# Expert weights split whole or in halves, none multiplied in float32, in a two-layer hybrid decoder trunk

## The chip, the cores and the metric

The kernel runs on one core of one Trainium2 chip. The metric is the device time of one execution in microseconds. The time before is 1491.45 us, the median of 3 runs (1490.14 to 1492.38). All runs are fp32 in and out.

## What is computed

Two layers, each a mixer (differential attention and a gated delta rule side by side), a normalisation, a channel mixer and a normalisation. The first layer's channel mixer is a dense SwiGLU, the second's is the part this document is about: 256 tokens, each sent to 2 of 8 experts.

```python
D_MODEL, SEQ, N_EXPERTS, TOP_K, D_FF_EXPERT = 1024, 256, 8, 2, 3584

def swiglu(x, w_gate, w_up, w_down):
    return (jax.nn.silu(x @ w_gate) * (x @ w_up)) @ w_down

def moe_ffn(x, router_w, w_gate, w_up, w_down):
    logits = jnp.einsum('td,de->te', xf, router_w)
    top_val, top_idx = lax.top_k(logits, TOP_K)
    gates = jax.nn.softmax(top_val, axis=-1)
    ...
    y = swiglu(xb, w_gate[e_b], w_up[e_b], w_down[e_b])
    ...
```

Here `xb` holds the tokens sorted by expert, in blocks that belong to one expert each, and a token's output is the sum of `gate * y` over its two experts.

## The kernel before

**Precision by two parts.** Weights and activations are fp32, and TensorE works on them as pairs of float32r numbers: a high part, which ScalarE (ACT) makes by a copy, and a low part, which VectorE (DVE) makes as the difference. `halves` (L162) does this to a loaded piece of weights: for each half of the piece an ACT copy `wh<-raw` (L177) and a DVE subtraction `wl<-raw,wh` (L180). A product is then x_high·w_high + x_low·w_high + x_high·w_low.

**The expert loop** (`experts`, L980). Each expert's 3584 hidden columns are taken in two chunks of 1792 (`CHUNK`). A chunk needs 8 gate pieces and 8 up pieces of 128 x 1792 (896 KB each) and 7 down pieces of 128 x 2048 (1 MB each). For each chunk the loop multiplies the 8 gate pieces (`in_pieces`, `products`), a few down pieces of the chunk before (`down`, through `more`), applies SiLU to the gate banks (ACT `hh<-ps`, L1194), multiplies the 8 up pieces, again a few down pieces of the chunk before, then DVE multiplies the up banks into `hh` (L1217), and the rest of the down pieces of the chunk before follow. So the down products of a chunk always run inside the chunk that comes after it. TensorE (PE) then transposes `hh` into `hT` (`to_features`, L1125), with one ACT copy and one DVE subtraction for each group of columns.

**Wide and narrow experts.** The experts run in an order by token count: a wide one (up to 128 rows), then narrow and wide in turn for three narrow ones (up to 64 rows, `NARROW = 3`, `TURN`), then two more wide ones. A wide expert multiplies a weight's high part by x_high and x_low and its low part by x_high. A narrow one puts x_high and x_low side by side as 64 + 64 rows, so a piece costs one pass for each part of the weight. The low rows' result then stands in the upper half of the PSUM banks. `leads` (L1114) copies these upper halves on ACT (`room<-ps`), and PE adds them to the lower halves by a product with `shift` (the "moves").

**The last gate and the last up piece of a narrow chunk are not split.** `load(..., whole=True)` puts them in a slot of their own (`ring2`), `as_one` (L1027) has made x in one part, and `products` multiplies them in float32 on the lower 64 rows alone. Since these four products don't touch the upper halves, the `room` copies stand ahead of them:

```python
if narrow and sub[0] == KD - 1:
    subs = next(downs, None)
    moves = leads(banks)
products(banks, xg, narrow, *sub, x32)
```

**Buffers.** Weights land in 7 raw slots (`RING`). The split parts have 4 half-piece buffers in `wpool` and 4 more in `wpool2`, taken in turn, so four pieces can be split ahead.

**What sets the order.** The instructions of each engine run in order. A list scheduler sets it ahead of time, from the order of the program, where nothing is pinned. `side` is a list of small steps, of which one is placed behind each piece: the transposes into `hT`, `combine` (L1088: the copy of an expert's result from PSUM into `ys`, its product with the transposed dispatch matrix `DT`, and the addition into `x_tok`), `transposed` (which makes `DT` from `D`) and `dispatch` (L1003: it gathers the rows of the next one or two experts into `xg`, eight parts, each with PE products into a bank `ps_a` and ACT copies `xg<-ps_a`). The tag `a` has two banks. `ys` and `D` share one buffer.

## Time and profile before

| | |
|---|---|
| median of 3 runs | 1491.45 us (1490.14 to 1492.38) |
| profiled execution | 1492.99 us |
| its span, first to last instruction | 1490.9 us |
| TensorE clock granted, mean | 0.988 |
| PE / PE weight loads / DVE / ACT busy | 1448.6 / 1233.1 / 1218.3 / 1036.6 us |
| HBM read | 431.17 MB, 290 GB/s over the span |

The profile shows one execution. Busy time counts the engine's instructions from start to end with overlaps taken once. Matmuls are pipelined, so PE's busy time overstates the work; the distance from one matmul's start to the next one's says what it costs. The expert loop runs from about 520 us to the end; what comes before it isn't touched by the change.

### The profile page before, as it was taken

The page shows a single profiled execution, that of the slowest core. Times are in us where ns is not written, and L with a number is a line of the kernel's source. Part 1 is how long each engine was busy: PE and PEld are TensorE (multiplying, and loading weights), DVE is VectorE, ACT ScalarE, POOL GpSimd, SP SyncE. Part 2 cuts the span into 40 slices and gives each one's busy share as a digit, 9 for nine tenths or more (in the row PEclk, how much of TensorE's full clock was granted, in tenths as well). Part 3 has the DMA queues.
Part 4 walks back from the last instruction along what each step waited for, and adds up shares of the span by engine and source line. Part 5 has one row for each costly group of instructions (what it writes and reads, how often), then busy time and mean ns, then how long its engine had stood idle before and what let it go on. Part 6 is the DMA issues. An engine that isn't in the chain of part 4 may idle for free.

```text
span 1490.9 us, 24038 instructions
## 1 busy us (share of the span) xinstructions
PE 1448.6 (97%) x8873; PEld 1233.1 (83%) x8873; DVE 1218.3 (82%) x1609; ACT 1036.6 (70%) x1553; POOL 23.7 (2%) x37
## 2 busy tenths in 40 slices
PE   8999999999999999999999999999999999999995
PEld 8978899998987889886698877588877589888884
DVE  6877655556796798989899989899989899989886
ACT  5748544456666587787797887886887877778763
POOL 1100000000000000000000000000000000000000
PEclk9999999999999999999999999999999999999998
DMA  9633455535533179999999999999999899999891
GB/s 322 219 106 118 153 195 195 193 121 196 193 113 100 54 298 363 386 371 374 380 394 384 375 390 394 356 393 408 352 379 417 335 395 413 338 357 395 292 394 34
DMA packets 89124, 433.93 MB, mean 291 GB/s; under 512 B 7816, under 2 KB 9992, under 8 KB 74912
## 3 DMA queue, kind: packets, MB, share of 16 engines
q1 hardware_dynamic: 87808, 428.54, 76.1%
q0 software_dynamic: 1184, 3.71, 0.9%
q8 instruction: 73, 1.20, 0.3%
q14 instruction: 59, 0.48, 0.1%
HBM read 431.17 MB, written 1.05 MB: 290 GB/s over the span
## 4 chain that ended last, share of the span: by engine, by line
PE 87%; DVE 7%; issue 2%; ACT 2%; DMA 0%; DVEq 0%; SPq 0%; ACTq 0%
PE ps_b L99 26%; PE ps_mm L99 25%; PE ps_gd L99 24%; PE ps_a L99 9%; DVE wl L180 4%; PE ps_a L1137 2%; ACT wh L177 1%; DVE x_in L1099 1%; PE ps_mm L566 0%; ACT junk L415 0%; DVE hT L1140 0%; ACT xT L240 0%; PE ps_gd L408 0%; PE ps_mm L670 0%; DVE D L999 0%
## 5 line engine op out<-in xcount | busy, mean ns | idle before, releaser
L180 DVE TENSOR_TENSOR wl<-raw,wh 128x896 fp32r<-128x896 f32 (+2 forms) x851 | 925.7, 1144 | 145.8 <-ACT wh L177 139.4
L177 ACT ACTIVATE wh<-raw 128x896 fp32r<-128x896 f32 (+2 forms) x851 | 792.4, 995 | 153.4 <-PE ps_gd L99 68.4
L99 PE MATMUL ps_b<-wh,hT 128*128 128x512 f32 x816 | 232.6, 396 | 0.7 <-ACT hT L1139 0.7
L99 PE MATMUL ps_gd<-wh,xg 128*128 128x448 f32 x808 | 218.8, 368 | 0.0
L99 PE MATMUL ps_mm<-wh,xg 128*128 128x448 f32 x808 | 212.5, 372 | 0.3
L99 PEld LDWEIGHTS ps_b<-wh,hT 128*128 128x128 f32 x816 | 152.0, 188 | 39.2 <-issue 6.4
L99 PEld LDWEIGHTS ps_gd<-wh,xg 128*128 128x128 f32 x808 | 151.9, 189 | 12.7
L99 PE MATMUL ps_b<-wl,hT 128*128 128x512 f32 x492 | 159.0, 400 | 2.2 <-DVE wl L180 2.2
L99 PEld LDWEIGHTS ps_mm<-wh,xg 128*128 128x128 f32 x808 | 147.6, 189 | 16.4 <-ACT wh L177 2.0
L99 PE MATMUL ps_gd<-wl,xg 128*128 128x448 f32 x488 | 142.9, 374 | 8.9 <-DVE wl L180 7.2
L99 PE MATMUL ps_mm<-wl,xg 128*128 128x448 f32 x488 | 140.7, 369 | 0.1
L99 PEld LDWEIGHTS ps_b<-wl,hT 128*128 128x128 f32 x492 | 90.9, 188 | 31.9 <-DVE wl L180 6.7
L99 PEld LDWEIGHTS ps_gd<-wl,xg 128*128 128x128 f32 x488 | 88.8, 188 | 27.7 <-DVE wl L180 20.2
L99 PEld LDWEIGHTS ps_mm<-wl,xg 128*128 128x128 f32 x488 | 90.9, 188 | 11.7 <-DVE wl L180 4.3
L1139 ACT ACTIVATE hT<-ps_a 128x512 fp32r<-128x512 f32 (+2 forms) x52 | 27.4, 544 | 64.8 <-PE ps_a L1137 37.7
L99 PE MATMUL ps_mm<-xT,wh 128*128 128x256 f32 x448 | 70.9, 280 | 0.0
L99 PEld LDWEIGHTS ps_mm<-xT,wh 128*128 128x128 f32 x448 | 60.8, 189 | 0.4
L1140 DVE TENSOR_TENSOR hT<-ps_a,hT 128x512 fp32r<-128x512 f32 (+2 forms) x52 | 31.8, 621 | 26.5 <-ACT hT L1139 26.5
L99 PE MATMUL ps_gd<-xT,wh 128*128 128x256 f32 x320 | 50.5, 280 | 0.0
L1092 ACT ACTIVATE ys<-ps_b 128x512 fp32r<-128x512 f32 x14 | 8.4, 599 | 53.2 <-PE ps_b L99 39.0
L99 PE MATMUL ps_mm<-xT,wl 128*128 128x256 f32 x224 | 44.6, 280 | 0.0
L99 PEld LDWEIGHTS ps_gd<-xT,wh 128*128 128x128 f32 x320 | 43.1, 189 | 0.0
(407 smaller groups left out, 1660.2 us busy)
## 6 DMA issues: line engine op xcount, KB each, us to landing
raw<-in_moe_w_gate_dram SPq DMA_DIRECT2D x128, 896.0 KB, 8.2
raw<-in_moe_w_up_dram SPq DMA_DIRECT2D x128, 896.0 KB, 6.6
raw<-in_moe_w_down_dram SPq DMA_DIRECT2D x110, 1024.0 KB, 8.1
raw<-in_w_in_dram SPq DMA_DIRECT2D x24, 1024.0 KB, 6.6
raw<-in_ffn_w_gate_dram SPq DMA_DIRECT2D x11, 1024.0 KB, 5.1
raw<-in_ffn_w_up_dram SPq DMA_DIRECT2D x11, 1024.0 KB, 5.1
raw<-in_ffn_w_down_dram SPq DMA_DIRECT2D x11, 1024.0 KB, 4.9
raw<-in_w_out_dram SPq DMA_DIRECT2D x8, 1024.0 KB, 4.9
```

What stands on the lines that cost most here:

```text
L99: return PE.matmul(o, lhsT, rhs, start=start, stop=stop, skip_group_check=True)
L177: high = S.activation(wh[:, c:c + n], w, AF.Copy)
L180: low = V.tensor_tensor(wl[:, c:c + n], w, wh[:, c:c + n].bitcast(F32), op=ALU.subtract)
L1092: S.activation(yh, py[i], AF.Copy)
L1099: V.scalar_tensor_tensor(o, pt, jobs[n][2][:, b], o, op0=ALU.mult, op1=ALU.add)
L1137: PE.transpose(pt[:, f * w:(f + 1) * w], hv[:, f0 + f], ident[rows, rows])
L1139: S.activation(hT[:, f0:f0 + n_, 0], pv, AF.Copy)
L1140: V.tensor_tensor(hT[:, f0:f0 + n_, 1], pv, hT[:, f0:f0 + n_, 0].bitcast(F32), op=ALU.subtract)
```

## The change

- No piece is multiplied in float32: `as_one` and the argument `whole` are gone, and a narrow chunk splits all 16 of its gate and up pieces.
- Every second piece of the expert loop is split in one go: one ACT copy and one DVE subtraction of 1792 or 2048 elements in place of two of half the size (`Whole`). `wpool2` now holds two buffers of 2048 in place of four of 1024. `products` and `down` treat a whole piece with all its high parts first, then its low parts.
- The extra raw slot takes every eighth load or the next gate or up piece after it, in wide and narrow chunks.
- `leads` now stands behind the last piece and behind the split of one down piece, since the last piece now writes the upper rows too.
- `combine` is cut in two: its copies stay behind the gate pieces, and its additions, `transposed` and the next `dispatch` stand behind the up pieces (`carry`). `ys` and `D` get two buffers.

```diff
-    def load(src, nk, cols, parts=1, cut=1, whole=False):
-        pool, size = (extra[0], CHUNK) if whole and extra else (ring, WC)
+    def load(src, nk, cols, parts=1, cut=1):
+        loads[0] += 1
+        pool, size = ring, WC
+        if extra and cols == CHUNK and loads[0] >= 8:
+            pool, size = extra[0], CHUNK
+            loads[0] = 0
...
+    def halves(ld, cut=1, count=2, parts=1):
+        raw, nk, cols = ld
+        if extra and cut == 1 and parts == 1:
+            turn[0] += 1
+            if turn[0] % 2 == 0:
+                n = nk * cols
+                wh = extra[1].tile([P, WC], F32R, tag="wh", name=nm("wh"))
+                wl = extra[1].tile([P, WC], F32R, tag="wl", name=nm("wl"))
+                high = S.activation(wh[:, :n], raw[:, :n], AF.Copy)
+                low = V.tensor_tensor(wl[:, :n], raw[:, :n], wh[:, :n].bitcast(F32), op=ALU.subtract)
+                return Whole((k, wh[:, k * cols:(k + 1) * cols], wl[:, k * cols:(k + 1) * cols]) for k in range(nk))
+        return split(ld, cut, count)
...
-        def products(outs, xg, narrow, k, parts, x32=None):
-            if narrow and k == KD - 1:
-                for i, o in enumerate(outs):
-                    mm(o[0:64], x32, parts[:, i * BANK:(i + 1) * BANK], False, False)
-                return
+        def products(outs, xg, narrow, k, parts):
             for i, (_, wh, wl) in enumerate(parts):
-                o = outs[2 * i:2 * i + 2]
+                m = 4 if isinstance(parts, Whole) else 2
+                o = outs[m * i:m * i + m]
...
-            return [lambda i=i: part(i) for i in range(2)]
+            return [lambda i=i: copy(i) for i in range(2)], [lambda i=i: add(i) for i in range(2)]
...
-                for sub in in_pieces(wg, c, len(first or ()), narrow):
-                    if narrow and sub[0] == KD - 1:
-                        subs = next(downs, None)
-                        moves = leads(banks)
-                    products(banks, xg, narrow, *sub, x32)
+                for sub in in_pieces(wg, c, len(first or ())):
+                    products(banks, xg, narrow, *sub)
...
+                subs = next(downs, None)
+                moves = leads(banks) if narrow else ()
                 more(subs)
...
+                side, carry = carry, []
                 if c == NC - 1 and groups and n + 1 not in xgs:
-                    group = groups.pop(0)
-                    tiles, side = dispatch([jobs[g] for g in group])
-                    xgs.update(zip(group, tiles))
+                    def gather(group=groups.pop(0), side=side):
+                        tiles, steps = dispatch([jobs[g] for g in group])
+                        xgs.update(zip(group, tiles))
+                        side.extend(steps)
+
+                    side.append(gather)
...
                 if pend and pend[1] == NC - 1:
-                    side += combine(pend[0], pend[3], DT)
+                    copies, carry = combine(pend[0], pend[3], DT)
+                    side += copies
                 if c == 0:
-                    side.append(lambda n=n, later=later: later.append(transposed(n)))
+                    carry.append(lambda n=n, later=later: later.append(transposed(n)))
```

The change also moves instructions, since the scheduler orders anew. In all the following places `wh` is a high part of weights. The first is ACT at the end of the gate pieces of the first chunk of the second narrow expert, before:

```order
L177 ACTIVATE wh_9075<-raw_9065 128x896
L177 ACTIVATE wh_9087<-raw_9085 128x1024
L177 ACTIVATE wh_9091<-raw_9085 128x1024
L1121 ACTIVATE room_9095<-ps_mm_8927 64x448
L1121 ACTIVATE room_9095<-ps_gd_8929 64x448
...
L177 ACTIVATE wh_9123<-raw_9121 128x1024
L177 ACTIVATE wh_9127<-raw_9121 128x1024
L177 ACTIVATE wh_9149<-raw_9147 128x1024
L177 ACTIVATE wh_9153<-raw_9147 128x1024
L1194 ACTIVATE hh_9104<-ps_mm_8927 64x448
L1194 ACTIVATE hh_9104<-ps_gd_8929 64x448
```

and after the change:

```order
L198 ACTIVATE wh_8865<-raw_8855 128x896
L180 ACTIVATE wh_8876<-raw_8874 128x2048
L1138 ACTIVATE room_8880<-ps_mm_8715 64x448
L1138 ACTIVATE room_8880<-ps_gd_8717 64x448
...
L198 ACTIVATE wh_8903<-raw_8901 128x1024
L198 ACTIVATE wh_8907<-raw_8901 128x1024
L1209 ACTIVATE hh_8873<-ps_mm_8715 64x448
L1209 ACTIVATE hh_8873<-ps_gd_8717 64x448
...
L180 ACTIVATE wh_8929<-raw_8927 128x2048
```

Between the four `room` copies and the four SiLUs one down piece is split now, where two were before, and the next one stands behind the SiLUs.

The second place is ACT at the start of the gate pieces of that expert's second chunk, before:

```order
L177 ACTIVATE wh_9439<-raw_9429 128x896
L1092 ACTIVATE ys_9503<-ps_b_8509 128x512
L177 ACTIVATE wh_9460<-raw_9458 128x896
L177 ACTIVATE wh_9468<-raw_9458 128x896
L177 ACTIVATE wh_9487<-raw_9485 128x896
L1139 ACTIVATE hT_9406<-ps_a_9447 128x8x64
L177 ACTIVATE wh_9495<-raw_9485 128x896
L1139 ACTIVATE hT_9406<-ps_a_9476 128x6x64
L177 ACTIVATE wh_9516<-raw_9514 128x896
L177 ACTIVATE wh_9524<-raw_9514 128x896
L1092 ACTIVATE ys_9532<-ps_b_8510 128x512
```

and after the change:

```order
L180 ACTIVATE wh_9195<-raw_9193 128x1792
L1156 ACTIVATE hT_9170<-ps_a_9207 128x8x64
L1156 ACTIVATE hT_9170<-ps_a_9236 128x6x64
L1106 ACTIVATE ys_9259<-ps_b_8304 128x512
L198 ACTIVATE wh_9220<-raw_9218 128x896
L198 ACTIVATE wh_9228<-raw_9218 128x896
L1106 ACTIVATE ys_9280<-ps_b_8305 128x512
L180 ACTIVATE wh_9247<-raw_9245 128x1792
```

Both `hT` copies stand ahead of the third gate piece, and on PE their transposes stand among the last down pieces of the chunk before, where they were behind the second and third gate pieces.

The third place is ACT at the end of a wide expert's second chunk, where `dispatch` gathers for the next two experts. Before, the eight parts stand behind the eight up pieces, one each; the last three are:

```order
L177 ACTIVATE wh_8824<-raw_8822 128x1024
L177 ACTIVATE wh_8828<-raw_8822 128x1024
L1023 ACTIVATE xg_8588<-ps_a_8757 128x128
L1023 ACTIVATE xg_8589<-ps_a_8757 128x256
L177 ACTIVATE wh_8846<-raw_8844 128x1024
L177 ACTIVATE wh_8850<-raw_8844 128x1024
L1023 ACTIVATE xg_8588<-ps_a_8786 128x128
L1023 ACTIVATE xg_8589<-ps_a_8786 128x256
L177 ACTIVATE wh_8872<-raw_8870 128x1024
L177 ACTIVATE wh_8876<-raw_8870 128x1024
L1023 ACTIVATE xg_8588<-ps_a_8815 128x128
L1023 ACTIVATE xg_8589<-ps_a_8815 128x256
```

After the change the fourth to the eighth part stand on PE behind the last up piece, the eighth behind one further matmul, and on ACT so:

```order
L1044 ACTIVATE xg_8482<-ps_a_8585 128x128
L1044 ACTIVATE xg_8482<-ps_a_8592 128x128
...
L180 ACTIVATE wh_8666<-raw_8664 128x2048
L1044 ACTIVATE xg_8482<-ps_a_8599 128x128
L1044 ACTIVATE xg_8482<-ps_a_8606 128x128
...
L198 ACTIVATE wh_8684<-raw_8682 128x1024
L198 ACTIVATE wh_8688<-raw_8682 128x1024
L1044 ACTIVATE xg_8482<-ps_a_8613 128x128
```

The eighth part (8613) takes the bank of the sixth (8599), whose copy now stands behind a whole down piece.

## Rows read from the trace of the kernel before

**Rows 1.** Busy time by engine, the whole span (busy us, share, count).

```profile
PE 1448.6 (97%) x8873; PEld 1233.1 (83%) x8873; DVE 1218.3 (82%) x1609; ACT 1036.6 (70%) x1553; POOL 23.7 (2%) x37
```

**Rows 2.** Four chunks in turn, from one multiplication into `hh` to the next.

```profile
core 0: us, PE busy (x) PEld busy (x) DVE busy (x) ACT busy (x) POOL busy (x), PEclk, DMA share, GB/s
849.28:906.91 57.63, 57.37 (x257) 44.63 (x255) 51.16 (x53) 48.76 (x64) 0.00 (x0) 1.00 1.00 395
906.91:965.14 58.23, 55.33 (x227) 38.46 (x227) 51.41 (x57) 44.30 (x59) 0.00 (x0) 1.00 0.93 363
965.14:1018.38 53.24, 53.24 (x256) 46.64 (x255) 50.47 (x51) 43.07 (x52) 0.00 (x0) 1.00 1.00 400
1018.38:1080.39 62.01, 61.46 (x309) 54.45 (x308) 57.99 (x65) 46.70 (x69) 0.00 (x0) 1.00 0.97 373
```

**Rows 3.** Chain that ended last, 849 to 966 us (start us, us, what).

```profile
900.68 1.65 PE ps_mm L99 x4
902.33 1.50 PE ps_gd L99 x4
...
915.57 0.81 PE ps_mm L99 x4
916.38 0.81 PE ps_gd L99 x4
```

**Rows 4.** Timeline of DVE, 849 to 966 us (start, us, instructions, idle before).

```profile
856.26 8.11 DVE L180 TENSOR_TENSOR wl<-raw,wh 128x896 fp32r<-128x896 f32 x8
866.55 0.69 DVE L1140 TENSOR_TENSOR hT<-ps_a,hT 128x512 fp32r<-128x512 f32 x1 [2.19 <-ACT hT L1139]
...
884.95 16.39 DVE L180 TENSOR_TENSOR wl<-raw,wh 128x896 fp32r<-128x896 f32 x16 [2.27 <-ACT wh L177]
902.36 4.63 DVE L180 TENSOR_TENSOR wl<-raw,wh 128x1024 fp32r<-128x1024 f32 x4 [1.02 <-ACT wh L177]
...
916.01 0.69 DVE L1093 TENSOR_TENSOR ys<-ps_b,ys 128x512 fp32r<-128x512 f32 x1 [0.62 <-ACT ys L1092]
...
920.55 0.69 DVE L1140 TENSOR_TENSOR hT<-ps_a,hT 128x512 fp32r<-128x512 f32 x1 [0.60 <-ACT hT L1139]
...
923.10 0.56 DVE L1140 TENSOR_TENSOR hT<-ps_a,hT 128x384 fp32r<-128x384 f32 x1 [0.62 <-ACT hT L1139]
923.93 1.09 DVE L180 TENSOR_TENSOR wl<-raw,wh 128x896 fp32r<-128x896 f32 x1 [0.28 <-ACT wh L177]
...
943.31 17.52 DVE L180 TENSOR_TENSOR wl<-raw,wh 128x1024 fp32r<-128x1024 f32 x17 [3.22 <-ACT wh L177]
```

**Rows 5.** Groups of DVE instructions by shape, 849.28 to 965.14 us (busy, mean | idle).

```profile
L180 DVE TENSOR_TENSOR wl<-raw,wh 128x896 fp32r<-128x896 f32 x56 | 57.5, 1086 | 3.0 <-ACT wh L177 2.6
L180 DVE TENSOR_TENSOR wl<-raw,wh 128x1024 fp32r<-128x1024 f32 x29 | 33.9, 1220 | 5.8 <-ACT wh L177 5.8
```

**Rows 6.** Groups of ACT splits by shape, 560 to 1470 us.

```profile
L177 ACT ACTIVATE wh<-raw 128x896 fp32r<-128x896 f32 x456 | 399.0, 951 | 14.6 <-PE ps_b L99 6.6 <-PE ps_gd L99 3.3 <-PE ps_mm L99 2.9
L177 ACT ACTIVATE wh<-raw 128x1024 fp32r<-128x1024 f32 x223 | 222.1, 1055 | 10.4 <-DMA raw<-in_moe_w_down_dram 4.5 <-PE ps_mm L99 3.0 <-PE ps_gd L99 1.6
```

**Rows 7.** Timeline of ACT, 849 to 966 us.

```profile
865.92 0.60 ACT L1139 ACTIVATE hT<-ps_a 128x512 fp32r<-128x512 f32 x1 [3.20 <-PE ps_a L1137]
...
933.16 0.97 ACT L1121 ACTIVATE room<-ps_mm 64x448 fp32r<-64x448 f32 x2 [2.00 <-PE ps_mm L99]
```

**Rows 8.** Waits of PE and its weight loads in a wide pair, 965.14 to 1080.39 us (total, times, longest).

```profile
PEld ps_b L99 <- DVE wl L180: 1.0, 2, 0.8
...
PE ps_b L99 <- DVE wl L180: 0.5, 1, 0.5
```

**Rows 9.** Timeline of ACT, 1018 to 1081 us.

```profile
1061.95 0.55 ACT L1023 ACTIVATE xg<-ps_a 128x128 fp32r<-128x128 f32 x2 [4.27 <-PE ps_a L99]
```

**Rows 10.** Chain that ended last, by a wide expert's last up pieces and at the tail.

```profile
847.79 0.43 PE ps_a L99 x4
...
1448.76 0.61 ACT hT L1139
```

More of the change, by code (lines that the diff above doesn't have):

```diff
@@ L160, in load, with split @@
         return raw, nk, cols
-    def halves(ld, cut=1, count=2):
+    class Whole(list):
+        pass
+    def halves(ld, cut=1, count=2, parts=1):
+        raw, nk, cols = ld
+        m = nk * cols // count
+        if extra and cut == 1 and parts == 1:
[5 more added lines that the diff above has]
+                high = S.activation(wh[:, :n], raw[:, :n], AF.Copy)
+                if fence_high[0] is not None:
+                    order(high, fence_high[0])
+                low = V.tensor_tensor(wl[:, :n], raw[:, :n], wh[:, :n].bitcast(F32), op=ALU.subtract)
+                if fence[0] is not None:
+                    order(low, fence[0])
+                return Whole((k, wh[:, k * cols:(k + 1) * cols], wl[:, k * cols:(k + 1) * cols]) for k in range(nk))
+        return split(ld, cut, count)
+    def split(ld, cut, count):
         raw, nk, cols = ld
@@ L185, in piece @@
     def piece(src, nk, cols, parts=1, cut=1):
-        return halves(load(src, nk, cols, parts, cut), cut)
+        return halves(load(src, nk, cols, parts, cut), cut, parts=parts)
     pre_ctx = ExitStack()
@@ L1063, in products @@
                 for w in (wh, wl):
-                    for j in range(2):
+                    for j in range(m):
                         mm(o[j], x_, w[:, j * BANK:(j + 1) * BANK], k == 0 and w is wh, False)
@@ L1070, in down_pieces @@
             for f in range(first, NF, 2):
[L1071 removed]
+                subs = piece(wd[:, f:f + 2, :], 2, D, parts, cut if f == NF - 2 else 1)
+                yield (Whole if isinstance(subs, Whole) else list)((f + j, wh, wl) for j, wh, wl in subs)
         def down(subs, n, c, hT, py):
[L1074 removed]
+            turns = [(sub[0], i, sub[i]) for sub in subs for i in (1, 2)]
@@ L1075, in down @@
+            if isinstance(subs, Whole):
+                turns.sort(key=lambda t: t[1])
+            for f, part, w in turns:
                 K, k = NC * NF, c * NF + f
+                last = k == K - 1 and part == 2
                 if jobs[n][3]:
                     x_ = hT[:, f].rearrange("p c s -> p (c s)")
-                    for w in (wh, wl):
+                    for i, o in enumerate(py):
+                        mm(o, x_, w[:, i * 512:(i + 1) * 512], k == 0 and part == 1, last)
+                else:
+                    for c_ in range(2 if part == 1 else 1):
@@ L1088, in combine, with copy, add @@
-        def combine(n, py, DT):
-            def part(i):
-                ys = mp.tile([P, 2, 512], F32R, tag="ys", name=nm("ys"))
-                yh, yl = ys[:, 0], ys[:, 1]
-                S.activation(yh, py[i], AF.Copy)
-                V.tensor_tensor(yl, py[i], yh.bitcast(F32), op=ALU.subtract)
+                            mm(o, hT[:, f, c_], w[:, i * 512:(i + 1) * 512], k == 0 and part == 1 and c_ == 0, last)
+        def combine(n, py, DT):
+            parts = []
+            def copy(i):
+                ys = mp.tile([P, 2, 512], F32R, tag="ys", name=nm("ys"), bufs=2)
+                S.activation(ys[:, 0], py[i], AF.Copy)
+                V.tensor_tensor(ys[:, 1], py[i], ys[:, 0].bitcast(F32), op=ALU.subtract)
+                parts.append(ys)
+            def add(i):
@@ L1160, in experts @@
             xg = xgs.pop(n)
-            x32 = as_one(xg) if narrow else None
             wg, wu = (weights(n, i).rearrange("(k p) c -> p k c", p=P) for i in range(2))
@@ L1210, in experts @@
                     side.pop(0)()
+                subs = next(downs, None)
+                moves = leads(banks) if narrow else ()
                 more(subs)
```

49 lines of the change are left out of this document (14 added, 35 removed).

## The prediction

> **What bounds the kernel now.** I read the busy times by engine first. TensorE is busy for 97% of the span, VectorE for 82% [rows 1], which looks like a kernel bound by TensorE. But that is a mean over stages, and it is overstated by pipelined matmuls, so the next view is the expert loop chunk by chunk. Four chunks repeat three times: the first and second chunk of a narrow expert (called N1 and N2 here), then those of a wide one (W1 and W2). They take 57.6, 58.2, 53.2 and 62.0 us [rows 2]. The granted clock is 1.00 in all of them, so the clock has no part in what follows. W1 moves 400 GB/s with its DMA engines busy all the time, and that is as good as a floor: no chunk with the same number of pieces can be much below 53 us.
>
> The reader is to see two things in these rows. VectorE is busy for 51.16 of N1's 57.63 us and 51.41 of N2's 58.23 us [rows 2], so it idles for 6.5 and 6.8 us, 13.3 us for a narrow expert. TensorE is the tighter engine in W2, with 61.46 of 62.01 us busy. The narrow chunks are thus bound by neither engine alone. They are a chain that passes from one to the other. The timeline of VectorE names where it idles: 2.19 us for the first `hT` copy, 2.27 us ahead of the up pieces and 1.02 us ahead of the last down split in N1; in N2 0.62, 0.60, 0.62 and 0.28 us around `ys` and `hT`, and 3.22 us at the SiLUs [rows 4].
>
> **TensorE's part.** A narrow gate piece in float32 costs 1.65 + 1.50 = 3.15 us, a split one 0.81 + 0.81 = 1.62 us [rows 3]. Each narrow expert has four of the former (two chunks, gate and up), so three experts have 12, and 12 x 1.53 = 18.4 us of work goes. I count none of it as gain: these pieces were the ones that VectorE didn't have to split, and it is VectorE on whose time the narrow chunks now stand. The 3.15 us were its cover.
>
> **VectorE's part.** Eight subtractions in sequence take 8.11 us [rows 4], so about 1.003 us from one start to the next, though one lasts 1.086 us [rows 5]. Four more pieces for an expert are 8 x 1.003 = +8.0 us. Splitting in one go saves what two instructions cost more than one. From 896 to 1024 elements a subtraction lasts 1220 - 1086 = 134 ns longer [rows 5], so 896 more elements add 134 x 7 = 938 ns. One of 1792 should then take 1.003 + 0.938 = 1.941 us from start to start against 2.006 for two, a saving of 0.065 us. A narrow expert's two chunks have 46 pieces, 23 of them in one go: -1.5 us. (The small addition of `as_one` is left out.) VectorE's work grows by 6.5 us for a narrow expert, 3.25 us a chunk. If its idle time stayed, three experts would lose 19.5 us. The question is how much of the 13.3 us goes.
>
> N1: The first `hT` copy on ScalarE waits 3.20 us for the transposes on TensorE [rows 7], and VectorE 2.19 us for it. The change puts the transposes earlier, among the last down pieces of the chunk before: -2.0 us. Against that, the split ahead of the last down piece now waits behind `room` copies that wait for the last piece; 1.02 us [rows 4] becomes about 1.8, since one `room` pair takes 0.97 us [rows 7]: +0.8. N1 changes by 3.25 - 2.0 + 0.8 = +2.05 us.
>
> N2: The four waits around `ys` and `hT` (2.12 us) should go, because `ys` has two buffers and the `hT` copies stand ahead of the third gate piece. Of the 3.22 us at the SiLUs I take 1.9 away: between the `room` copies and the SiLUs stands one down piece where two stood, and VectorE comes there later by what it has more to do. With the small waits I leave 2.0 us of 6.8: -4.8. N2 changes by 3.25 - 4.8 = -1.55 us. A narrow expert: **+0.5 us**, and its idle time falls from 13.3 to 7.3 us. Three: +1.5 us.
>
> **Wide chunks.** TensorE's wait for a low part costs up to 0.8 us in a pair [rows 8]; it comes from ScalarE standing still at the single `ys` buffer, and the change gives two. Once per W2, and there are four second chunks of wide experts that dispatch: -3.2 us. The dispatch itself is a new cost. Each of its eight parts is 0.43 us on TensorE [rows 10], and they stood one behind each up piece. Now three stand there and five come together behind the last up piece. The eighth takes the bank of the sixth, whose ScalarE copies now stand behind the split of a whole down piece. A whole copy of 2048 should last 1055 + 8 x 104 = 1.89 us, with 104 ns being the step from 951 to 1055 ns [rows 6]. The bounds for TensorE's stall are nothing (ScalarE has got to it in time; it idles 4.27 us ahead of these copies at the start of this row of parts now [rows 9]) and 1.89 + 0.55 us for the split and the copies [rows 6, 9]. I take 1.0 us in the mean, rather under the middle since ScalarE runs ahead: four times, +4.0 us, range 0 to +9.8.
>
> **The rest.** At the tail `hT` stands in the chain with 0.61 us [rows 10]; earlier transposes take it out: -0.6. The eighth load in the spare slot: nothing. In N2 and W2 the DMA engines aren't full (0.93 and 0.97), and in W1, where they are, TensorE is busy for all of the 53.24 us too [rows 2]. Were loads late, ScalarE would wait for them; its down splits wait 4.5 us for DMA in the whole loop [rows 6], which is all that there is to gain. Splitting in one go in wide chunks: VectorE has 2.8 and 4.0 us of idle there, TensorE hides it. It has a price where TensorE waits for a piece: its first product starts up to 0.94 us later. That bound is kept for the range.
>
> **Sum.** 1.5 - 3.2 + 4.0 - 0.6 = +1.7 us on the profiled execution's 1492.99 us, which is 1.54 us above the median of the runs shown. On the median that is 1491.45 + 1.7, given as **1493.0 us**. A measurement of this kernel can tell about 0.2%, 3 us, from no change, so this forecast is "no change".
>
> **Rivals.**
>
> *Faster, idle time falls further (1484 us).* In W1 VectorE idles for 2.8 us, with TensorE and DMA full. If N1 and N2 come to the like, a narrow expert's idle is 5.5 us, not 7.3: -1.8 x 3 = -5.4. And if ScalarE gets to the dispatch copies in time, -4.0 goes too: 1493.0 - 9.4 = 1483.6. For it: every wait named in the rows of N2 is for ScalarE, which is the least busy of the three (48.76 and 44.30 us [rows 2]). Against it: whole copies make ScalarE's answers later. Chance 0.32.
>
> *Faster, one go saves more (1487 us).* What if a subtraction pays in sequence all of the 0.157 us by which two lone halves exceed a lone whole (2 x 1.086 against 2.02 us)? Then 23 pieces save 2.1 us more for a narrow expert, 6.3 in all: 1486.7. The row of eight in 8.11 us [rows 4] speaks against it, as only 8 x 1.003 pass there, not 8 x 1.086. [...] Chance 0.08.
>
> *Slower, whole copies and late `room` copies stop VectorE (1505 us).* The place is the end of the gate and of the up pieces of a narrow chunk. ScalarE may copy `room` only when TensorE has done the last piece, and the SiLUs stand behind another split. VectorE, with no float32 piece as cover, waits for all of it, and where the next piece is whole for a copy 0.94 us longer. If the `hT` and `ys` waits go (2.0 + 2.1) but the SiLU wait of 3.22 stays and two of the four places cost a further 0.94 us, the idle left is 13.3 - 4.1 + 1.9 = 11.1 us, 3.8 more than in my sum: 1493.0 + 3 x 3.8 = 1504.4. It decides from where a narrow expert keeps over 7.8 us of idle. For it: the 3.22 and the 2.27 us are already of this kind. Against it: a VectorE that is later by 3 us meets a ScalarE that has gone on. Chance 0.31.
>
> That the edits don't do what they say I rule out: the order of instructions shows the splits of 1792 and 2048 and no product of unsplit weights.
>
> **How the numbers follow.** My sum has 0.29, the rivals 0.32, 0.08 and 0.31. Faster is 0.32 + 0.08 = 0.40, same 0.29, slower 0.31. The range takes in the first rival, and the last with the upper bound of the dispatch in part: 1481 to 1507 us.
>
> **What would show it.** Right: N1 near 59.7 us, N2 near 56.7, VectorE's idle in both together near 7.3 us, whole subtractions near 2.02 us long, TensorE waiting about 1 us for a bank behind the last up piece of W2, no wait of a `ys` copy for TensorE. Wrong: idle under 6 or over 8 us in a narrow expert; a W2 with no stall or one over 2 us; whole subtractions that follow each other at other than 1.94 us; or a N1 or N2 in which TensorE, not VectorE, is full.

## The result: slower by 0.9%, inside the range, and not by the sum that was forecast

| | before | changed |
|---|---|---|
| median of 7 runs | 1490.34 us | 1502.62 us |
| lowest to highest | 1490.01 to 1492.38 us | 1499.54 to 1510.21 us |
| ratio | | 1.0086, 95% interval 1.0066 to 1.0106 |
| span of the profiled execution | 1490.9 us | 1501.4 us |

The forecast was 1493.0 us, "no change", with a range of 1481 to 1507. The time lies in the range, and on the side of the last rival (1505 us); the change for the worse is clear of the noise. The busy times of the changed kernel, to be read beside [rows 1]:

```profile
PE 1433.2 (95%) x8873; PEld 1236.5 (82%) x8873; DVE 1226.7 (82%) x1448; ACT 1039.2 (69%) x1395; POOL 23.8 (2%) x37
```

TensorE lost 15.4 us of busy time, VectorE gained 8.4 us, and the span still grew by 10.5 us: what left TensorE came back as waiting. The same four chunks as in [rows 2], from one multiplication into `hh` to the next (columns as there):

```profile
851.84:911.48 59.64, 56.01 (x258) 45.36 (x257) 52.10 (x43) 50.06 (x59) 0.00 (x0) 1.00 0.95 353
911.48:970.17 58.69, 52.89 (x228) 39.46 (x226) 55.34 (x51) 46.05 (x50) 0.00 (x0) 0.97 0.96 367
970.17:1024.12 53.95, 53.14 (x250) 46.80 (x250) 50.59 (x41) 43.72 (x43) 0.00 (x0) 0.97 0.99 403
1024.12:1088.07 63.95, 62.77 (x314) 55.12 (x312) 56.98 (x55) 45.45 (x54) 0.00 (x0) 1.00 0.96 375
```

N1 went from 57.63 to 59.64 us, N2 from 58.23 to 58.69, W1 from 53.24 to 53.95, W2 from 62.01 to 63.95. TensorE now idles 3.6 us in N1, 5.8 in N2 and 1.2 in W2, where it idled 0.3, 2.9 and 0.6 (span less PE busy in these rows). VectorE idles 7.5 us in N1 and 3.35 in N2, 10.9 for a narrow expert where it was 13.3. A second thing is new: the granted clock of N2 and W1 reads 0.97, where all four were at 1.00.

The whole difference of the two profiled spans, +10.5 us, adds up from the chunks, by the starts of the multiplications into `hh`: the first chunk of the loop +4.6 (40.0 us from its first product to there before, 526.79 to 566.76; 44.6 now, 524.03 to 568.58; each with one stretch of some 3 us in it in which the granted clock was 0.50, from 527 us before and from 548.5 now); the three narrow experts -0.3, +2.5 and +1.8; the three W1 together +0.6; the three W2 +4.9; the last expert's two chunks -0.8; what follows them +0.1; and what comes ahead of the loop's first product -2.8, code that the change doesn't touch. That is 10.6. At the tail one line of the chain that ended last is as it was in [rows 10]:

```profile
1459.17 0.61 ACT hT L1156
```

Of the whole some 3.9 us are the clock, an estimate from the same chunks with and without a fall in them: N2 takes 58.69 us here and 58.0 in the two other narrow experts, W1 53.95 and 53.8 against 52.3. Without falls W1 would be 0.8 us shorter than before each time. The other executions fit this: their mean granted clock is 0.988 over the seven of the changed kernel, and 0.991 over the 35 of the kernel before that were taken beside run twelve.

**Where VectorE waits now.** Its timeline in N1 and N2 (start, us, instructions, idle before them):

```profile
858.43 2.02 DVE L183 TENSOR_TENSOR wl<-raw,wh 128x1792 fp32r<-128x1792 f32 x1
860.37 2.08 DVE L201 TENSOR_TENSOR wl<-raw,wh 128x896 fp32r<-128x896 f32 x2
862.83 2.03 DVE L183 TENSOR_TENSOR wl<-raw,wh 128x1792 fp32r<-128x1792 f32 x1 [0.38 <-ACT wh L180]
...
867.35 2.02 DVE L183 TENSOR_TENSOR wl<-raw,wh 128x1792 fp32r<-128x1792 f32 x1 [0.48 <-ACT wh L180]
...
871.23 0.69 DVE L1157 TENSOR_TENSOR hT<-ps_a,hT 128x512 fp32r<-128x512 f32 x1 [1.26 <-ACT hT L1156]
...
886.85 2.29 DVE L183 TENSOR_TENSOR wl<-raw,wh 128x2048 fp32r<-128x2048 f32 x1 [2.23 <-ACT wh L180]
...
909.27 2.29 DVE L183 TENSOR_TENSOR wl<-raw,wh 128x2048 fp32r<-128x2048 f32 x1 [2.10 <-ACT wh L180]
...
943.30 2.29 DVE L183 TENSOR_TENSOR wl<-raw,wh 128x2048 fp32r<-128x2048 f32 x1 [1.43 <-ACT wh L180]
946.77 2.36 DVE L201 TENSOR_TENSOR wl<-raw,wh 128x1024 fp32r<-128x1024 f32 x2 [1.18 <-ACT wh L198]
```

The first two rows give the price of one go: 858.43 to 860.37 is 1.94 us from start to start. The 2.27 and 3.22 us at the SiLUs in [rows 4] have become 2.23 and 1.43 + 1.18 us, and the 1.02 us ahead of N1's last down pieces are 2.10. The three longest now end on the copy of a whole down piece. The waits around `ys` and `hT` in N2 (2.12 us) are gone; the one of N1 (2.19 us) is spread over 0.38, 0.48, 1.26, 0.39 and 0.17 us. The timeline of ACT shows the first `hT` copy that still waits in N1, and what the copy of a down piece stands behind:

```profile
868.50 0.60 ACT L1156 ACTIVATE hT<-ps_a 128x512 fp32r<-128x512 f32 x1 [1.19 <-PE ps_a L1154]
...
905.47 0.97 ACT L1138 ACTIVATE room<-ps_mm 64x448 fp32r<-64x448 f32 x2 [3.67 <-PE ps_mm L99]
906.34 0.97 ACT L1138 ACTIVATE room<-ps_gd 64x448 fp32r<-64x448 f32 x2
907.33 1.91 ACT L180 ACTIVATE wh<-raw 128x2048 fp32r<-128x2048 f32 x1
```

ScalarE stands still for 3.67 us until TensorE has done the last up piece, copies `room` for 1.86 us, and copies a whole down piece for 1.91; VectorE gets it at 909.27.

**Where TensorE waits in W2.** Its timeline from W2 into the next N1:

```profile
1060.69 1.21 PE L99 MATMUL ps_b<-wl,hT 128*128 128x512 f32 x4 [0.98 <-DVE wl L183]
...
1086.77 1.14 PE L99 MATMUL ps_a<-D,xs 128*128 128x192 f32 x8 [0.20 <-ACT xg L1044]
1087.74 0.42 PE L99 MATMUL ps_b<-wh,hT 128*128 128x512 f32 x1
1089.45 0.69 PE L99 MATMUL ps_a<-D,xs 128*128 128x192 f32 x4 [1.29 <-ACT xg L1044]
```

The bunched dispatch parts cost 0.20 + 1.29 us, the last of them at the bank that the prediction named. And a down piece's first product with its low part waits 0.98 us for a whole subtraction, where [rows 8] had 0.5. The rest of W2's +1.9 us is mostly no wait: its window holds five more matmuls than before (x314 and x309 in the rows of chunks), about 1 us by the 0.2 us from one product to the next in [rows 3] (one lasts 0.37 us, the mean of 808 products `ps_mm<-wh,xg` before, so they overlap), so the mark between W2 and N1 has moved too.

**Where TensorE waits for low parts in the whole loop** (560 to 1470 us: total us, times, longest), before:

```profile
PE ps_gd L99 <- DVE wl L180: 7.2, 11, 1.2
PE ps_b L99 <- DVE wl L180: 2.2, 4, 0.6
```

and after the change, with its waits for the dispatch:

```profile
PE ps_mm L99 <- DVE wl L183: 21.4, 33, 1.5
PE ps_b L99 <- DVE wl L183: 6.9, 9, 1.0
PE ps_a L99 <- ACT xg L1044: 3.3, 5, 1.3
```

The waits for low parts were 9.4 us and are 28.3 us now for the subtractions in one go (L183) alone.

### The profile page after: what moved, and what is told of

It reads as the page before. It is cut to its first block, busy times and chain, and to the rows that moved or that the text cites. A ratio compares the mean times of both kernels' runs of the same rounds, so it can differ in the third digit from the quotient of the medians.

```text
span 1501.4 us, 23569 instructions
## 1 busy us (share of the span) xinstructions
PE 1433.2 (95%) x8873; PEld 1236.5 (82%) x8873; DVE 1226.7 (82%) x1448; ACT 1039.2 (69%) x1395; POOL 23.8 (2%) x37
## 4 chain that ended last, share of the span: by engine, by line
PE 45%; DVE 11%; ACT 5%; issue 4%; DVEq 0%; ACTq 0%
PE ps_mm L99 15%; PE ps_gd L99 14%; PE ps_b L99 14%; DVE wl L183 5%; DVE wl L201 4%; ACT wh L180 2%; ACT wh L198 1%; PE ps_a L99 1%; PE ps_a L1154 1%; ACT room L1138 1%; DVE hh L1234 1%; DVE x_in L1116 1%; ACT xg L1044 0%; DVE ys L1107 0%; ACT hh L1209 0%
## 5 line engine op out<-in xcount | busy, mean ns | idle before, releaser
L201 DVE TENSOR_TENSOR wl<-raw,wh 128x896 fp32r<-128x896 f32 (+2 forms) x511 | 572.7, 1151 | 111.5 <-ACT wh L198 106.9
L198 ACT ACTIVATE wh<-raw 128x896 fp32r<-128x896 f32 (+2 forms) x511 | 496.2, 1003 | 136.8 <-PE ps_gd L99 66.9
L183 DVE TENSOR_TENSOR wl<-raw,wh 128x1792 fp32r<-128x1792 f32 (+1 forms) x182 | 382.0, 2099 | 54.8 <-ACT wh L180 54.8
L180 ACT ACTIVATE wh<-raw 128x1792 fp32r<-128x1792 f32 (+1 forms) x182 | 321.5, 1767 | 41.4 <-PE ps_gd L99 30.8
L99 PE MATMUL ps_mm<-wh,xg 128*128 128x448 f32 x832 | 228.1, 370 | 3.6 <-ACT hh L1209 2.8
L99 PE MATMUL ps_gd<-wh,xg 128*128 128x448 f32 x832 | 227.9, 368 | 0.0
L99 PE MATMUL ps_b<-wh,hT 128*128 128x512 f32 x816 | 225.8, 398 | 0.7 <-ACT hT L1156 0.7
L99 PE MATMUL ps_mm<-wl,xg 128*128 128x448 f32 x512 | 150.1, 374 | 21.5 <-DVE wl L183 21.4
L99 PE MATMUL ps_b<-wl,hT 128*128 128x512 f32 x492 | 152.4, 408 | 7.6 <-DVE wl L183 6.9
L99 PEld LDWEIGHTS ps_mm<-wl,xg 128*128 128x128 f32 x512 | 92.5, 188 | 43.9 <-DVE wl L183 35.5
L99 PEld LDWEIGHTS ps_gd<-wl,xg 128*128 128x128 f32 x512 | 94.5, 188 | 10.9 <-DVE wl L201 1.2
```

Of the source, the lines that this page charges most:

```text
L99: return PE.matmul(o, lhsT, rhs, start=start, stop=stop, skip_group_check=True)
L180: high = S.activation(wh[:, :n], raw[:, :n], AF.Copy)
L183: low = V.tensor_tensor(wl[:, :n], raw[:, :n], wh[:, :n].bitcast(F32), op=ALU.subtract)
L198: high = S.activation(wh[:, c:c + n], w, AF.Copy)
L201: low = V.tensor_tensor(wl[:, c:c + n], w, wh[:, c:c + n].bitcast(F32), op=ALU.subtract)
```

## The experiments

Two theories stood at the start. The first was the last rival: VectorE has more to do and waits at the `room` copies. The second: splits in one go and the bunched dispatch make TensorE wait. In all runs the ratio is to the kernel before on the same chip; the intervals are about 0.15 to 0.25% to either side. Two chips were used, so runs are compared with each other by their ratios.

**One: halves again.**

```diff
-        if extra and cut == 1 and parts == 1:
+        if False:
...
-            wh = wpool.tile([P, WH], F32R, tag="wh", name=nm("wh"))
-            wl = wpool.tile([P, WH], F32R, tag="wl", name=nm("wl"))
+            pool, size = wpool, WH
+            if extra:
+                turn[0] += 1
+                if turn[0] % 2 == 0:
+                    pool, size = extra[1], 1024
+            wh = pool.tile([P, size], F32R, tag="wh", name=nm("wh"))
+            wl = pool.tile([P, size], F32R, tag="wl", name=nm("wl"))
...
-tc.tile_pool(name="wpool2", bufs=2, reuse_waits="tile") as wpool2
+tc.tile_pool(name="wpool2", bufs=4, reuse_waits="tile") as wpool2
```

> The changed kernel with every piece split in two halves again (the four half-size buffers back); all else stays. If the splits in one go cost the time (TensorE waits for whole low parts, 42.4 us of waits in 71 cases in the changed kernel between 560 and 1470 us, weight loads and products together, and in W2 one of about 2 us), W2 falls by 1 to 2 us and the kernel to about 1496 us, 0.4% over the kernel before. If they cost nothing and save VectorE 0.065 us a piece, it rises by 23 x 0.065 = 1.5 us for each narrow expert, 4.5 us in all, to about 1507 us.

Measured: 1.0025 (1.0008 to 1.0042), median 1495.26 us. The same four chunks:

```profile
852.70:909.71 57.01, 55.34 (x253) 44.37 (x253) 52.94 (x55) 50.39 (x70) 0.00 (x0) 1.00 0.95 360
909.71:969.12 59.41, 55.45 (x231) 38.67 (x230) 56.01 (x61) 47.94 (x63) 0.00 (x0) 1.00 0.95 371
969.12:1021.24 52.12, 51.50 (x251) 45.36 (x250) 51.34 (x54) 44.27 (x54) 0.00 (x0) 1.00 1.01 406
1021.24:1085.23 63.99, 63.24 (x316) 55.55 (x314) 57.79 (x65) 46.41 (x65) 0.00 (x0) 1.00 0.99 387
```

Undoing one part gives back 0.6 of the 0.86%, so the splits in one go are the larger part of the loss. But not where it was expected: W2 stays at 64 us. The largest single place is the loop's first chunk, with 38.8 us (527.53 to 566.36) in place of 44.6: the stop of TensorE that run five shows below isn't there. N1 falls by 2.6 us. Of the 1.8 us by which W1 falls, 1.7 are the clock, as an undisturbed W1 of the changed kernel takes 52.3 us; and N2 rises by 1.4 against an undisturbed N2 (58.0 us), not by 0.7. TensorE's waits for low parts are back at 9.5 us:

```profile
PE ps_gd L99 <- DVE wl L206: 5.7, 20, 0.3
PE ps_b L99 <- DVE wl L206: 2.8, 6, 0.5
PE ps_mm L99 <- DVE wl L206: 1.0, 6, 0.2
```

(The 42.4 us in the expectation add 35.5 us of weight loads to 6.9 of products.) VectorE's busy time in the four chunks is 218.07 us here (52.94 + 56.01 + 51.34 + 57.79) and 215.01 in the changed kernel, 3.06 us for 46 pieces in one go, or 0.067 each. The price of the prediction was right; the saving is real and doesn't pay.

**Two: float32 for the last pieces again.** `as_one`, `whole`, the extra slot for them and the early `room` copies are put back as in the kernel before:

```diff
+                subs, moves = None, ()
-                for sub in in_pieces(wg, c, len(first or ())):
-                    products(banks, xg, narrow, *sub)
+                for sub in in_pieces(wg, c, len(first or ()), narrow):
+                    if narrow and sub[0] == KD - 1:
+                        subs = next(downs, None)
+                        moves = leads(banks)
+                    products(banks, xg, narrow, *sub, x32)
...
```

> The changed kernel with the last gate and up piece of a narrow chunk in float32 again (with as_one, their slot and the room copies ahead of them); splits in one go, the cut combine and the later dispatch stay. If VectorE's added work and its idle time at the room copies are the loss, the narrow experts get shorter by 1 to 2.5 us each and the clock stays up: about 1497 us, 0.45% over the kernel before. If the dispatch and the whole splits are the loss, W2 stays at 63.5 to 65 us and the time stays within 3 us of 1502.

Measured: 1.006 (1.0039 to 1.0081), median 1499.68 us. The interval overlaps that of the changed kernel, so this run alone shows no gain. W2 stays at 63.95 us. N1 is 58.28, N2 58.19. The clock didn't stay up, as the first theory expected: at the stop in the first chunk this profile has a clock of 0.50 from 550 to 556 us. VectorE's added work is not what cost most.

**Three: dispatch early.** `combine`'s additions and `transposed` go back behind the gate pieces, and `dispatch` starts behind the first up piece:

```diff
-                    copies, carry = combine(pend[0], pend[3], DT)
-                    side += copies
+                    for copy_, add_ in zip(*combine(pend[0], pend[3], DT)):
+                        side.append(lambda copy_=copy_, add_=add_: (copy_(), add_()))
...
-                    carry.append(lambda n=n, later=later: later.append(transposed(n)))
+                    side.append(lambda n=n, later=later: later.append(transposed(n)))
...
-                    def gather(group=groups.pop(0), side=side):
...
-                    side.append(gather)
+                    group = groups.pop(0)
+                    tiles, side = dispatch([jobs[g] for g in group])
+                    xgs.update(zip(group, tiles))
```

> The changed kernel with copies and additions of combine together behind the gate pieces and the dispatch behind the up pieces from the first on, one part each, as before; two buffers for ys and D stay. If the bunched dispatch costs the wide experts their time (TensorE waits 1.29 us for a bank at the start of N1, and W2 is 1.1 to 1.9 us longer), W2 returns to 62 us and N1 loses 1 us: 4 x 2 = 8 us less, about 1495 us. If the additions behind the gate pieces then stop VectorE in N2, N2 grows by up to 2 us in each of three narrow experts and the gain halves: about 1500 us.

Measured: 1.0045 (1.003 to 1.0059), median 1497.84 us, clear of the changed kernel. The first and the last of the four chunks:

```profile
852.95:913.24 60.29, 57.41 (x265) 46.38 (x263) 52.23 (x44) 49.61 (x55) 0.00 (x0) 1.00 0.96 369
...
1024.27:1085.32 61.05, 61.05 (x308) 53.94 (x307) 57.21 (x54) 45.75 (x58) 0.00 (x0) 1.00 0.98 378
```

W2 is full again, at 61.05 us, 2.9 less. N1 takes 0.65 us of it back. What was expected of W2 came; N2 is 58.63 us, 0.6 over an undisturbed N2 of the changed kernel, where up to 2 were expected.

**Four: `room` copies first.**

```diff
-                subs = next(downs, None)
                 moves = leads(banks) if narrow else ()
+                subs = next(downs, None)
```

> The changed kernel with the room copies ahead of the split of the next down piece, directly behind the last gate or up piece. If VectorE idles at the end of the gate and of the up pieces because SiLU and splits stand behind room copies that come late (2.23 and 2.10 us in N1, 1.43 and 1.18 us in N2), the waits get shorter by about 1 us in each place, 4 us for a narrow expert, unless VectorE then waits for the split behind them: about 1491 us if so. If the wait only changes its place, no change: 1502 us within 3.

Measured: 1.0138 (1.0115 to 1.0161), median 1511.78 us, the slowest of all. N1 is 60.62, N2 60.20. VectorE's timeline at the end of its N2:

```profile
974.46 2.29 DVE L183 TENSOR_TENSOR wl<-raw,wh 128x2048 fp32r<-128x2048 f32 x1 [2.71 <-ACT wh L180]
```

The changed kernel waits 0.53 us there. With `room` ahead, no down piece is copied while ScalarE waits for the last up piece, so VectorE has nothing behind that piece. The theory that late `room` copies are the fault and earlier ones the cure is dropped: by this trace VectorE is better served there by a piece split ahead of them.

**Five: one go alone, in the kernel before.** `Whole`, `halves`, `products`, `down` and `wpool2` as in the change's diff, nothing else.

> The kernel before with one part of the change alone: every second split piece in one go (two buffers of 2048 in place of four of 1024). By the prediction's price VectorE saves 0.065 us for each such piece and the kernel gets 3 to 4 us faster or stays (1487 to 1491). If whole splits are the change's loss (undoing them in the changed kernel gave 0.6% back), it gets slower by 6 to 9 us, to about 1498 us, with the first chunk of the loop longer than 50 us and VectorE idle ahead of whole subtractions.

Measured: 1.0039 (1.0024 to 1.0055), median 1497.58 us. Slower, as the second theory expected. Its first chunk takes 42.7 us from the first product to the multiplication into `hh`, with the clock at 1.00 from 523 to 570 us (40.0 before, with its stretch at 0.50), and not over 50 as expected. Its timelines of TensorE and ACT there:

```profile
550.93 0.67 PE L99 MATMUL ps_mm<-wh,xg 128*128 128x448 f32 x2 [2.83 <-ACT hh L1213]
```

```profile
547.32 1.70 ACT L174 ACTIVATE wh<-raw 128x1792 fp32r<-128x1792 f32 x1 [1.08 <-PE ps_gd L99]
549.04 1.28 ACT L1213 ACT_TABLE_LOAD   x1
550.33 0.98 ACT L1213 ACTIVATE hh<-ps_mm 128x448 f32<-128x448 f32 x2
```

The copy of the next whole piece waits 1.08 us for its buffer, takes 1.70 us, and stands ahead of the SiLUs. The first chunk has no down products to put in between, so TensorE stops for 2.83 us. The changed kernel has the same stop:

```profile
547.15 0.67 PE L99 MATMUL ps_mm<-wh,xg 128*128 128x448 f32 x2 [2.83 <-ACT hh L1209]
```

In the kernel before, TensorE's weight loads waited 0.4 us there.

**Six: halves and dispatch early.** Edits one and three together.

> The changed kernel with splits in halves and with the dispatch early, that is, without these two parts. If the two losses add (each undone alone gave 0.6% and 0.4% back), about 1489 us, no different from the kernel before within 0.2%. If N1 takes back what W2 gives, since combine's steps stand behind its gate pieces again (60.3 us with the dispatch early alone), it stays at about 1495 us.

Measured: 1.0016 (0.9998 to 1.0034), median 1494.42 us. No longer told from the kernel before, though all pieces are still split: the loss, as far as it can be measured, lies in these two parts. The two together are 0.70%, against 0.61 and 0.41 for each alone; with intervals of this width it isn't shown that they overlap. The last three of the four chunks:

```profile
909.24:969.29 60.05, 55.23 (x231) 38.70 (x230) 56.09 (x61) 47.92 (x63) 0.00 (x0) 1.00 0.95 366
969.29:1021.39 52.10, 51.49 (x251) 45.35 (x250) 51.33 (x54) 44.46 (x54) 0.00 (x0) 1.00 1.01 412
1021.39:1083.38 61.99, 61.89 (x309) 54.17 (x308) 57.98 (x65) 46.63 (x69) 0.00 (x0) 1.00 0.98 377
```

What is left of the change costs N2 1.8 us against the kernel before, and W1 gives back 1.1. Splitting all pieces is part of that, and no run tests it by itself. W2 is at 61.99 us, the 62.01 of before, with two `ys` buffers.

**Seven and eight: two steps behind each of the first four up pieces**, in the changed kernel, and in it with halves.

```diff
-                    if side:
-                        side.pop(0)()
+                    for _ in range(2 if sub[0] < 4 else 1):
+                        if side:
+                            side.pop(0)()
```

> The changed kernel, but behind each of the first four up pieces two of the small steps instead of one, so that the eight dispatch parts stand behind the second to the eighth up piece and none behind the last in a bunch; combine's additions stay behind up pieces. If the bunch is W2's loss, W2 falls from 63.4 to about 61 us and N1, with no steps of combine behind its gate pieces, stays under 60 us: 4 x 2.5 = 10 us less, about 1493 us. If the additions are W2's loss wherever they stand among the up pieces, W2 stays over 63 us and the time at 1500 us or above.

> Both of it: splits in halves, and two small steps behind each of the first four up pieces. If both losses are as thought and independent, 1502.6 - 9 - 10 = about 1484 us, faster than the kernel before by 0.4%. If VectorE is what is left as the bound in the narrow chunks (N2 59.4 us with halves), only the wide chunks gain and it comes to 1488 to 1491 us, no change against the kernel before.

Measured: 1.0054 (1.0037 to 1.0071), median 1500.34 us, and with halves 1.0014 (1.0 to 1.0028), median 1493.29 us. The interval of the first overlaps that of the changed kernel, so its gain stands on the profile alone. There the four chunks have no wait of TensorE for `xg` any more, but W2 falls only from 63.95 to 63.59 us and N1 from 59.64 to 58.56. Together that is 1.4 us, which is the stop of 0.20 + 1.29 us and no more. The 0.98 us at the down piece's low part stays. Run three has to be read over W2 and N1 together as well: its W2 holds six matmuls fewer than the changed kernel's and its N1 seven more (x308 and x265 against x314 and x258). Over both it gives back 2.2 us, so the bunch is about two thirds of that. In run three TensorE waits nowhere in W2, so the 0.98 us is gone with the additions moved; that these cause it is likely and not shown. The hoped-for 1484 us was missed by 9 us.

**Nine to twelve: which property of one go costs.** These start from run five. A piece for `wpool2` keeps the one large buffer, and `goes` decides if it is filled by one copy and one subtraction or by two of each:

```diff
-                high = S.activation(wh[:, :n], raw[:, :n], AF.Copy)
...
+                for i in range(1 if goes[0] else count):
+                    s = slice(0, n) if goes[0] else slice(i * m, (i + 1) * m)
+                    high = S.activation(wh[:, s], raw[:, s], AF.Copy)
...
+                if not goes[0]:
+                    return [(i * (nk // count), wh[:, i * m:(i + 1) * m], wl[:, i * m:(i + 1) * m]) for i in range(count)]
...
+                goes[0] = False                        # nine
+                goes[0] = n + c > 0                    # ten
+                goes[0] = not narrow and n + c > 0     # eleven
+                goes[0] = not narrow and c == 1        # twelve
```

A piece filled by halves is also multiplied by halves again, as the returned list isn't a `Whole`.

> The kernel before with the buffers of the splits in one go (two of 2048, one for every second piece), but each of those pieces still split by two copies and two subtractions of half the size. If the loss of the splits in one go (e5, 0.4% over the kernel before) is the coarser buffer, which comes free only when the whole piece has been multiplied, this kernel is as slow, about 1497 us. If it is the one long instruction (the copy of 1.70 us in the way of SiLU, and a first product that waits for the whole low part), the loss goes: 1491 us within 2.

> The kernel before with splits in one go everywhere but in the first chunk of the expert loop, where the same buffers are filled by halves. In e5 that chunk ended 4 us later than before, with TensorE stopped for 2.83 us at the SiLUs. If that is the long copy ahead of the SiLUs, 4 us come back and the time is about 1493.5 us, within 0.2% of the kernel before. If it is the buffers, the chunk stays 4 us longer and the time at 1497 us.

> As e10, but splits in one go in the chunks of wide experts alone; the narrow ones are split by halves into the same buffers. By the chunks of e5 (W1 0.3 us and W2 0.7 us shorter than before, the last chunks 1 us in all, N1 and N2 1.1 us longer each) this would take the gains without the losses: 1491 - 4 = about 1487 us. If the coarser buffers are what makes N1 and N2 longer, these stay at 58.7 and 59.4 us and it comes to 1493 us.

> As e11, but splits in one go only in the second chunks of wide experts. If W2's 0.7 us in e5 come from its own whole splits, W2 is 60.9 to 61.3 us here too and the rest as in e9: 3 to 4 us under e9. If they come from what stands ahead of W2 in W1, W2 is as before, 62.0 us, and the time that of e9.

Measured, median and ratio: nine 1491.64 us, 0.9993 (0.9978 to 1.0008); ten 1492.62 us, 1.0009 (0.9993 to 1.0024); eleven 1491.24 us, 0.9999 (0.9982 to 1.0015); twelve 1491.87 us, 1.0001 (0.9985 to 1.0017). None differs from the kernel before.

Nine shows that the coarser buffers, filled by halves, cost nothing. Ten gets back most of run five's loss (0.39% against 0.09%) by an edit to the first chunk alone: in the profiles that chunk takes 38.6 us in place of 42.7, and the stop of 2.83 us is gone. Of TensorE's waits at the SiLUs one row is left:

```profile
PEld ps_mm L99 <- ACT hh L1219: 0.5, 1, 0.5
```

ScalarE's timelines say what differs. Counted from the loop's start, ScalarE copies twelve pieces ahead of the first chunk's SiLUs in the six kernels whose first chunk is split in one go (the changed one and runs two to five and seven), and all six have the stop of 2.83 us. In the eight others it copies eleven, and none has it. In run ten the twelfth piece stands behind the SiLUs:

```profile
546.97 0.98 ACT L1219 ACTIVATE hh<-ps_mm 128x448 f32<-128x448 f32 x2
547.83 0.99 ACT L1219 ACTIVATE hh<-ps_gd 128x448 f32<-128x448 f32 x2
548.68 1.81 ACT L177 ACTIVATE wh<-raw 128x896 fp32r<-128x896 f32 x2
```

Two half copies take 1.81 us there and one whole copy 1.70, so it isn't the length of the copy that stops TensorE but the place that the scheduler gives to it.

The chunks behind the first stay as in run five (N1 58.7, N2 59.4 us), and with the wide chunks' gains the time isn't told from the kernel before. Eleven has W2 at 61.26 us (62.01 before), as hoped, but W1 at 53.84 (53.24), so it is no faster kernel (1487 us were expected). Twelve shows that W2's gain isn't W2's own: with one go there alone it is 62.6 us. No kernel of this study beats the one before.

## Why the prediction was right in its range and wrong in its sum

That the time lies in the range is luck in good part. The range was 26 us wide, faster had a chance of 0.40 and slower 0.31, and the last rival's 1504.4 us comes near the measured time with other terms: the first chunk (+4.6 us), the clock (about 3.9) and, but for +0.8 us, W2 (+4.9) weren't in it.

- **VectorE's price of one go: right.** 1.941 us from start to start was worked out, 1.94 is shown; 2.02 us long was expected, and the group of 121 such subtractions has a mean of 2018 ns. The rival that one go saves 0.157 us a piece is out: 0.067 us was measured between the changed kernel and run one. No row and no run shows the 0.157 us: by an estimate from [rows 5] a lone whole takes 1.086 + 0.938 = 2.024 us, 0.148 less than two lone halves, and in the changed kernel (560 to 1470 us) two halves at a mean of 1084 ns exceed one whole at 2018 ns by 0.150 us. In sequence two halves cost 0.067 us more than one whole, less than half of that.
- **VectorE's work for a narrow expert: right but for the chunks' ends.** +6.5 us was forecast. N1 and N2 together show 107.44 us busy against 102.57, +4.9. Of the 1.6 us between, 1.1 is half a down piece: 29 half subtractions of down pieces lie in the two chunks before, and now 14 halves and 7 wholes.
- **Its idle time: wrong.** "Its idle time falls from 13.3 to 7.3 us" is the step that failed; it fell to 10.9. N2's part came (3.35 us, and 2.7 without a fall of the clock; 2.0 expected). N1's didn't: +0.8 us at the last down piece became +1.1, and the -2.0 us at `hT` was only a change of place. The order that showed the `hT` copies earlier was that of a second chunk. In N1 they still stand among the gate pieces and wait for TensorE's transposes, 1.19, 0.66 and 0.64 us. A narrow expert was to cost +0.5 us. It cost -0.3, +2.5 and +1.8. The last rival's 11.1 us of idle was met almost to the figure, yet its +3.8 us for a narrow expert was too high, and run four shows that its cause, `room` copies that come too late, isn't the one to mend.
- **W2, the ys buffer: wrong.** "-3.2 us" from the second `ys` buffer didn't come. The 0.8 us behind it was a wait of the weight loads; TensorE's own was 0.5 [rows 8]. With two buffers and early dispatch (run six) TensorE doesn't wait for a low part in W2, and W2 is 61.99 us, as before.
- **W2, the dispatch: right in place and near in size.** 1.0 us each was taken, +4.0 us in all; 0.20 + 1.29 us is shown in one place and 3.3 us in the whole loop, and run seven gets 1.4 us back by taking the bunch away.
- **Whole pieces: the bound that was kept at nothing.** "It has a price where TensorE waits for a piece: its first product starts up to 0.94 us later" was put into the range and not the sum. It is there with 0.98 us in W2, where 0.5 stood, and over the loop with 28.3 us of waits for low parts in place of 9.4.
- **The first chunk: not seen.** The words were "Splitting in one go in wide chunks: ... TensorE hides it". In the loop's first chunk no down products are there to hide it, and 4.6 us go. Run ten shows it for the kernel before with one go; in the changed kernel it is the same stop of 2.83 us, and run one, without it, takes 38.8 us there in place of 44.6.
- **The tail: wrong.** -0.6 us was expected. What follows the last multiplication into `hh` takes 55.2 us where it took 55.1, and the `hT` copy still stands in the chain that ended last, with its 0.61 us.
- **The clock: wrong.** That "the clock has no part in what follows" held for the kernel before; in the changed one it has some 3.9 us (see the last section).

What stays open: why the scheduler takes a twelfth piece ahead of the SiLUs when it is split in one go, and how the loss of one go behind the first chunk divides between the order in which the scheduler then places copies and the long copies themselves. Each edit moves both.

## What to carry to other kernels

A saving on an engine that is waited for at one point and waits at the next is worth its price only if the waits don't grow with it: here 0.067 us a piece were saved and more than paid back, by copies that came to stand ahead of something short and urgent (the stop of 2.83 us in the first chunk) and by products that waited for whole low parts (28.3 us where it was 9.4). When an edit changes the size of instructions, compare the order on each engine at the urgent places, and not only the prices. Look for the stage that lacks the cover which the others have (the first chunk has no down products of a chunk before), and price the edit there by itself. Work that is spread one step to a piece was best left spread here: five steps behind the last piece stopped TensorE for 0.20 + 1.29 us.

## What was not expected of the hardware

TensorE's granted clock fell inside the expert loop, which it didn't do in the profiled execution of the kernel before between 540 and 1470 us (1.00 over that stretch). Stretches of the changed kernel (columns as in the chunks above; the clock is the number ahead of the DMA share):

```profile
545.00:547.00 2.00, 0.00 (x0) 0.00 (x0) 2.00 (x3) 1.97 (x4) 0.00 (x0) 1.00 1.02 419
548.50:551.50 3.00, 3.00 (x10) 2.65 (x9) 1.58 (x3) 1.86 (x2) 0.00 (x0) 0.50 1.01 418
```

```profile
938.00:940.00 2.00, 1.01 (x5) 0.95 (x6) 2.00 (x3) 0.50 (x2) 0.00 (x0) 1.00 1.01 405
941.00:944.00 3.00, 3.00 (x7) 1.52 (x6) 1.57 (x3) 2.95 (x4) 0.00 (x0) 0.50 1.03 411
944.00:946.00 2.00, 2.00 (x9) 1.09 (x8) 1.59 (x1) 1.43 (x4) 0.00 (x0) 0.91 0.70 290
```

In the first pair TensorE did nothing for 2 us (the stop at the SiLUs), and from 548.5 to 551.5 it ran at a granted clock of 0.50, while it was busy all the time. In the second it was busy for 1.01 of 2 us, and then at 0.50 for 3 us. Two more such stretches lie at the starts of W1 (0.50 from 975.5 to 978.5 us and from 1211 to 1214). The W1 with a fall take 53.95 and 53.8 us, the one without 52.3, so a fall costs about 1.5 us there, an estimate from these three.

What brings a fall isn't shown. The stop of 2.83 us is followed by one in the changed kernel and in runs two and seven (0.50 from 550 to 556 and from 550 to 552 us), and by none in runs three, four and five (1.00 from 545 to 593 us). Ahead of the first of the two falls in W1 TensorE stood still for 0.45 and 0.36 us, and for no longer in its timeline from 966 us on:

```profile
972.42 1.84 PE L1154 MATMUL ps_a<-cst,hh 64*128 64x64 f32 x14 [0.45 <-DVE hh L1234]
974.62 1.69 PE L99 MATMUL ps_b<-wl,hT 128*128 128x512 f32 x4 [0.36 <-DVE wl L183]
```

One pattern runs through the profiles. In six of the seven kernels that split all pieces the clock was 0.50 inside N2 or around the start of W1: from 941, 975.5 and 1211 us in the changed kernel, from 740 in runs one and six, at 950 in run three, from 977 in run four and from 972 in run eight. For run seven no such stretch is shown; its N2 and W1 from 914.56 to 1024.96 us are at 1.00. So is the kernel before, and so are N2 and W1 between 904 and 1027 us in runs two, five and eleven, all of which keep the float32 pieces. That is one profile of each kernel, and an observation, not a cause. For a prediction it means that a term can come up, here about 1.5 us each time, that no busy time of the kernel before contains.
